# A second group pair by half products in three feed-forwards, products in another order, packed setup loads, and collecting copies on ScalarE

## Chip, cores and metric

One NeuronCore of a Trainium2 chip runs the whole program. The time is device microseconds of one execution. The kernel before takes 1335.24 us, the median of 3 runs (1333.88 to 1336.06).

## The reference

Two layers over 256 tokens of width 1024, in float32. Each layer has two feed-forwards (width 2816), three attention branches (differential, sparse, windowed) whose outputs are gated and merged, and a gated embedding term. The change touches the feed-forwards and the constants that the attention needs:

```python
def swiglu(x, wi, wo):
    gate, up = jnp.split(x @ wi, 2, axis=-1)
    return (jax.nn.silu(gate) * up) @ wo
...
for i in range(DEPTH):
    h = h + 0.5 * swiglu(rms_norm(h, norm_g[i, 0]), ffn1_wi[i], ffn1_wo[i])
    ...   # three attention branches, merged, added to h
    h = h + 0.5 * swiglu(rms_norm(h, norm_g[i, 2]), ffn2_wi[i], ffn2_wo[i])
    h = h + jax.nn.sigmoid(rms_norm(h, norm_g[i, 3]) @ w_ple_gate[i]) * (p[i] @ w_ple[i])
```

## The kernel before

A float32 product is made of three matmuls: each operand is split into a rounded high part and the remainder (`split`, L228 on ScalarE and L223 on VectorE), and `mul3` adds high by high, high by low and low by high (L235, L236, L237). Each weight comes from memory once as a tile of 128x1024 (512 KB, tile `raw`, four buffers); ScalarE writes its high part `wh`, VectorE the low part `wl` (six buffers each). So VectorE and ScalarE each do one instruction per weight tile before TensorE may use it.

A feed-forward has 11 groups of 256 gate and 256 up columns. The 256 tokens are two blocks t of 128. A plain group is 4 lines, one per weight tile; a line is 12 matmuls of 512 columns (2 depth blocks, 2 token blocks, 3 parts). Groups 8 and 9 are made together by half products (`Seven`, `seven`): the products of a 2x2 block matrix by 7 instead of 8 block products, each 4 depth blocks x 3 parts, again 12 matmuls. For these VectorE subtracts weight tiles from one another (`minus`; `x` and `y` are held tiles of two weight tiles each, filled through the GpSimd queue, L296), and adds the results (`plus`, L611, L624). `lines` says by a list `kinds` in which order lines of plain groups (0) and half products (1) come.

Each line's result goes through `gated`: Silu on ScalarE (`act`, L547), a multiplication on VectorE (L549), and, once 512 columns are there, `turn_by_dma`: ScalarE puts the two 16-bit halves of the numbers apart (`cut`, L516), the SP queue transposes them by DMA (`flip`, L517), VectorE puts them together (`whole`, L521) and `split` makes `gT`, the operand of the second product `fo`. `setup` loads constants and is run beside the lines of the first feed-forward at three fixed lines.

A planner with its own idea of time sets the order of the instructions on each engine; engines, and the SP queue that issues nearly all transfers, work strictly in that order.

Of the kernel before, what the change touches and what calls it, by code (L numbers as in the profile page):

```python
# [32 lines left out]
WBUFS = 6  # L33
PACE_A, PACE_B, PACE_C = 0.75, 0.72, 0.6
# [41 lines left out]
def _stream(i, x):  # L76
# [4 lines left out]
    def ffn(n, wi, wo):  # L81
        for f in range(FG):
            s = slice(256 * f, 256 * f + 256)
            yield f"{n}{f}", _subs(np.concatenate([wi[:, :DFF][:, s], wi[:, DFF:][:, s]], 1), 2)
        for c in range(2):
            yield f"{n}o{c}", _subs(wo[:, 512 * c:512 * c + 512], 2)
# [49 lines left out]
def _constants():  # L136
# [16 lines left out]
            "fold": np.tile(np.eye(32, dtype=np.float32), (2, 1))}  # L153

# [32 lines left out]
def trunk(ctx: ExitStack, tc: tile.TileContext, a: dict, out: bass.AP, index: list):  # L187
# [88 lines left out]
    class Seven:  # L276


        order = ("11", "t1", "t2", "t3", "22", "21", "t4")

        def __init__(self, i, fa, fb, x, y):
# [3 lines left out]
            self.at = {}  # L285

# [5 lines left out]
        def fill(self, n, into=None):  # L292
            f, first = self.src[n]
            p = where[self.i, f][0] + first
            if into is not None:
                nc.gpsimd.dma_start(into.rearrange("p (j n) -> p j n", j=2), a["wst"][p:p + 2].rearrange("j p n -> p j n"))  # L296
# [8 lines left out]
        def minus(self, n, x, y):  # L305
            self.raw[n] = self.raw[y]
            for j in range(2):
                sub(self.raw[y][j], self.raw[x][j], self.raw[y][j])

        def make(self, n):  # L310
            if n == "11":
                self.fill("11", self.x())
            elif n == "t1":
                self.fill("12", self.y())
                self.minus("t1", "12", "11")
# [3 lines left out]
            elif n == "t3":  # L319
                self.minus("t3", "22", "12")  # L320
            elif n == "21":
                self.fill("21")
            elif n == "t4":
                self.minus("t4", "21", "t2")
            self.tiles[n] = []
            for raw in self.raw[n]:
# [3 lines left out]
                self.tiles[n].append((hi, lo))  # L330

# [178 lines left out]
    def turn_by_dma(pool, src, m):  # L510
# [3 lines left out]
        flip = pool.tile([128, 2, 4, 128], U16, tag="flip", bufs=3, name="flip")  # L514
# [4 lines left out]
        def collect():  # L519
# [6 lines left out]
    def ffn(i, n, norm, after, aside=None):  # L526
# [10 lines left out]
        def collect(t, all=False):  # L537
            while pending[t] and (all or pending[t][0][0] <= now[0]):
                _, first, m, whole = pending[t].pop(0)
                split(gT[t][:, 0, first:first + m, :], gT[t][:, 1, first:first + m, :], whole())  # L540

        def gated(f, t, x):
            first = f - f % 2
            if (first, t) not in held:
                held[first, t] = [pool.tile([128, 512], F32, tag="gated", bufs=4, name="gated"), 0]
            act = pool.tile([128, 256], F32, tag="act", bufs=3, name="act")
            nc.scalar.activation(act, x[:, :256], AF.Silu, scale=norm.r(t))  # L547
            to = held[first, t]
            nc.vector.tensor_tensor(to[0][:, 256 * (f % 2):256 * (f % 2) + 256], act, x[:, 256:], op=ALU.mult)  # L549
            to[1] += 1  # L550
            if to[1] == 2 or f == FG - 1:
                pending[t].append((now[0] + 3, 2 * first, 2 * to[1], turn_by_dma(pool, to[0], 2 * to[1])))

        def gathered(t, k):
            if k == 8:
                collect(t, True)
# [46 lines left out]
        def seven(fa, fb, w):  # L603
# [10 lines left out]
            p1, p5, p6, p7 = y_bank("p1"), tp_bank("p5"), tp_bank("p6"), tp_bank("p7")  # L614
# [8 lines left out]
            with tc.high_priority(offset=150):  # L623
                nc.vector.tensor_tensor(v, v, p6, op=ALU.add)  # L624
            yield
            times(p7, sums[3], "t3", True)
            with tc.high_priority(offset=150):
                x = plus("w", v, p7)
                gated(fb, 1, plus("c22", x, p5))
            yield  # L630
# [804 lines left out]
```

## Time and profile before

| | |
|---|---|
| median of 3 runs | 1335.24 us |
| the profiled execution | 1335.53 us, span 1333.8 us |
| TensorE busy | 99%, 6366 matmuls |
| VectorE, ScalarE busy | 75%, 63% |
| VectorE busy in the lines of the second feed-forward | 94.19 of 117.90 us |

The span is the time from the first to the last instruction; 1.7 us of the execution lie around it. A matmul's busy time in the profile (some 390 ns) overlaps that of its neighbours, so the distance between two starts is the measure of TensorE's speed, not the busy time. In the same way an instruction of VectorE or ScalarE starts before the one ahead of it has ended.

### The profile page before, as it was taken

What the parts mean: (1) busy time and instruction counts of PE and PEld (TensorE: products, weight loads), DVE (VectorE), ACT (ScalarE), POOL (GpSimd) and SP (SyncE); (2) the same over time, 40 slices, a digit from 0 to 9 for tenths busy, and PEclk for the clock granted to TensorE, in tenths of its full rate; (3) what the DMA queues carried; (4) which work ended last, traced back from release to release, by engine and by line L of the source; (5) the groups of instructions that cost most, each with busy time, mean ns of one, the idle gap of its engine ahead of it and who ended that gap; (6) DMA issues with size and microseconds to landing.
All of it is one profiled execution on the core that took longest, in us unless ns stands there. A gap on an engine that the chain in (4) does not pass through costs nothing.

```text
span 1333.8 us, 17981 instructions
## 1 busy us (share of the span) xinstructions
PE 1314.9 (99%) x6366; PEld 1082.6 (81%) x6366; DVE 1004.5 (75%) x1693; ACT 834.5 (63%) x1375; POOL 28.6 (2%) x44
## 2 busy tenths in 40 slices
PE   9999999999999999999999999999999999999997
PEld 6868888887887788888888888888888878888886
DVE  7868756668979787776788776667688888868665
ACT  6657645659757575664666665467695656657544
POOL 1000000000000000000000000000000000000000
PEclk9999999999999999999999999999999999999999
DMA  8658855355653575786666685744546436668762
GB/s 333 186 167 252 250 194 202 131 174 175 213 171 111 172 223 158 226 241 192 209 204 190 205 244 189 243 152 150 185 154 219 157 95 224 189 184 223 237 213 71
DMA packets 120327, 257.12 MB, mean 193 GB/s; under 512 B 55280, under 2 KB 60836, under 8 KB 120238
## 3 DMA queue, kind: packets, MB, share of 16 engines
q1 hardware_dynamic: 117310, 245.95, 59.4%
q0 software_dynamic: 2496, 9.47, 2.1%
q8 instruction: 50, 0.82, 0.3%
q10 hardware_dynamic: 432, 0.56, 0.1%
q14 instruction: 39, 0.32, 0.1%
HBM read 243.33 MB, written 1.08 MB: 183 GB/s over the span
## 4 chain that ended last, share of the span: by engine, by line
PE 88%; DVE 4%; DMA 3%; ACT 2%; issue 2%; SPq 0%; POOLq 0%; POOL 0%; DVEq 0%; ACTq 0%
PE ff L236 8%; PE ff L237 8%; PE ff L235 8%; PE fo L235 6%; PE fo L237 6%; PE fo L236 6%; PE gate L235 3%; PE gate L237 3%; PE gate L236 3%; DMA raw<-in_wst 3%; PE s L725 2%; DVE wl L223 2%; PE A L237 2%; PE A L235 2%; PE A L236 2%
## 5 line engine op out<-in xcount | busy, mean ns | idle before, releaser
L223 DVE TENSOR_TENSOR wl<-raw,wh 128x1024 fp32r<-128x1024 f32 (+2 forms) x432 | 520.0, 1212 | 164.5 <-ACT wh L228 158.9
L228 ACT ACTIVATE wh<-raw 128x1024 fp32r<-128x1024 f32 (+2 forms) x432 | 450.4, 1049 | 240.4 <-DMA raw<-in_wst 86.8
L236 PE MATMUL ff<-wl,nT 128*128 128x512 f32 x576 | 225.4, 393 | 1.2 <-DVE wl L223 1.1
L237 PE MATMUL ff<-wh,nT 128*128 128x512 f32 x576 | 224.2, 391 | 0.6 <-DVE nT L223 0.6
L235 PE MATMUL ff<-wh,nT 128*128 128x512 f32 x576 | 221.9, 392 | 2.6 <-ACT wh L228 1.7
L237 PE MATMUL fo<-wh,gT 128*128 128x512 f32 x352 | 133.8, 390 | 0.0
L236 PE MATMUL fo<-wl,gT 128*128 128x512 f32 x352 | 133.7, 390 | 0.0
L235 PE MATMUL fo<-wh,gT 128*128 128x512 f32 x352 | 133.1, 391 | 0.0
L236 PEld LDWEIGHTS ff<-wl,nT 128*128 128x128 f32 x576 | 108.7, 189 | 26.7 <-DVE wl L223 3.6
L235 PEld LDWEIGHTS ff<-wh,nT 128*128 128x128 f32 x576 | 108.4, 189 | 27.0 <-ACT wh L228 3.1
L237 PEld LDWEIGHTS ff<-wh,nT 128*128 128x128 f32 x576 | 108.7, 189 | 23.2 <-DVE nT L223 0.9
L237 PEld LDWEIGHTS fo<-wh,gT 128*128 128x128 f32 x352 | 66.1, 188 | 13.6
L236 PEld LDWEIGHTS fo<-wl,gT 128*128 128x128 f32 x352 | 66.1, 188 | 13.5
L235 PEld LDWEIGHTS fo<-wh,gT 128*128 128x128 f32 x352 | 66.1, 188 | 13.5
L235 PE MATMUL gate<-wh,nT 128*128 128x512 f32 x192 | 76.8, 400 | 0.0
L236 PE MATMUL gate<-wl,nT 128*128 128x512 f32 x192 | 76.3, 397 | 0.0
L237 PE MATMUL gate<-wh,nT 128*128 128x512 f32 x192 | 75.9, 395 | 0.0
L736 ACT ACTIVATE p<-p,st 128x128 f32<-128x128 f32 (+1 forms) x128 | 56.6, 446 | 6.3 <-DVE st L734 6.0
L228 ACT ACTIVATE gT<-whole 128x512 fp32r<-128x512 f32 (+1 forms) x48 | 28.3, 589 | 36.3 <-DVE whole L521 36.2
L521 DVE COPY whole<-flip 128x1024 uint16<-128x1024 uint16 (+1 forms) x48 | 33.9, 706 | 21.2 <-DMA flip<-cut 20.9
L516 ACT ACTIVATE cut<-gated 128x1024 uint16<-128x1024 uint16 (+1 forms) x48 | 44.7, 976 | 1.1 <-DVE gated L549 0.6
L235 PEld LDWEIGHTS gate<-wh,nT 128*128 128x128 f32 x192 | 36.1, 188 | 8.3 <-ACT wh L228 0.3
(339 smaller groups left out, 2367.7 us busy)
## 6 DMA issues: line engine op xcount, KB each, us to landing
raw<-in_wst SPq DMA_DIRECT2D x422, 512.0 KB, 4.4
band<-table SPq DMA_DIRECT2D x10, 512.0 KB, 5.0
x<-in_wst POOLq DMA_DIRECT2D x4, 1024.0 KB, 7.4
y<-in_wst POOLq DMA_DIRECT2D x4, 1024.0 KB, 7.1
raw<-in_wbv SPq DMA_DIRECT2D x4, 420.0 KB, 3.2
xt<-in_xt SPq DMA_DIRECT2D x4, 256.0 KB, 5.3
raw<-in_wst SPq DMA_DIRECT2D x4, 256.0 KB, 4.5
h<-in_x SPq DMA_DIRECT2D x2, 512.0 KB, 7.7
```

The costliest lines, as they stand in the source:

```text
L223: nc.vector.tensor_tensor(o, x, y, op=ALU.subtract)
L228: nc.scalar.activation(hi, src, AF.Copy)
L235: nc.tensor.matmul(ps, xh, wh, start=start, stop=False, **kw)
L236: nc.tensor.matmul(ps, xh, wl, start=False, stop=False, **kw)
L237: nc.tensor.matmul(ps, xl, wh, start=False, stop=stop, **kw)
L516: nc.scalar.activation(cut.rearrange("p (w n) -> p w n", w=2), halves(src)[:, :128 * m].rearrange("p n w -> p w n"), AF.Copy)
L521: tc.keep_in_program_order(nc.vector.tensor_copy(halves(whole)[:, :128 * m].rearrange("p n w -> p w n"), flip.rearrange("p (w a) b -> p w ...
L725: nc.tensor.matmul(o, q[r, x, qb[m], t * 128:(t + 1) * 128], kk, start=x + y == 0, stop=x == 1)
L736: nc.scalar.activation(p[j], p[j], AF.Exp, bias=st[:, j:j + 1], scale=-1.0, accum_out=st[:, n + j:n + j + 1])
```

## The change

- The weights of a pair of groups are stored as 512 gate columns and 512 up columns, so Silu and the multiplication work on 512 columns (`opened_by`, `closed`); group 10 stays as it was.
- In the three feed-forwards without `setup` two pairs, groups 2, 3 and 4, 5, are made by half products; in the first one, as before, the pair 8, 9.
- The order of the seven products is 11, t1, t2, 22, t3, 21, t4. Block 12 is filled ahead into the held tile y (`begin`; SP queue in the first feed-forward, GpSimd queue in the others), block 11 comes as ordinary raw tiles, and t1 is written to x. Another bank and a sum `u` are used. `spread` places the half products among the plain lines by a list of VectorE costs.
- `collect` waits five lines instead of three, takes what `fo` needs next, and the copy `whole` runs on ScalarE except near the end of the lines.
- Nine setup loads become two (`late`, `kept`), and setup's parts are run at lines 10, 25 and 35 instead of 17, 22 and 33.

```diff
     class Seven:
-        order = ("11", "t1", "t2", "t3", "22", "21", "t4")
+        order = ("11", "t1", "t2", "22", "t3", "21", "t4")
+        then = {"11": ("t1", "12", "11"), "22": ("t3", "22", "12"), "21": ("t4", "21", "t2")}
...
+        def begin(self):
+            self.fill("12", self.y())
...
         def minus(self, n, x, y):
-            self.raw[n] = self.raw[y]
+            into = [self.x()[:, SUB * j:SUB * j + SUB] for j in range(2)] if n == "t1" else self.raw[y]
             for j in range(2):
-                sub(self.raw[y][j], self.raw[x][j], self.raw[y][j])
+                sub(into[j], self.raw[x][j], self.raw[y][j])
+            self.raw[n] = into
...
+            if n in self.then:
+                self.minus(*self.then[n])
+            if n == "t3" and self.following:
+                self.following.begin()
@@
-            tc.keep_in_program_order(nc.vector.tensor_copy(
-                halves(whole)[:, :128 * m].rearrange("p n w -> p w n"), flip.rearrange("p (w a) b -> p w (a b)", w=2)))
+            tc.keep_in_program_order(nc.vector.tensor_copy(to, of) if late else nc.scalar.activation(to, of, AF.Copy))
@@
+        def opened_by(f, t, x):
+            held[f // 2, t] = pool.tile([128, 512], F32, tag="gated", bufs=5, name="gated")
+            m = 256 if f == FG - 1 else 512
+            nc.scalar.activation(held[f // 2, t][:, :m], x[:, :m], AF.Silu, scale=norm.r(t))
+
+        def closed(f, t, x):
+            g, m = held.pop((f // 2, t)), 256 if f == FG - 1 else 512
+            nc.vector.tensor_tensor(g[:, :m], g[:, :m], x[:, 512 - m:], op=ALU.mult)
+            pending[t].append((now[0] + 5, 4 * (f // 2), m // 128, turn_by_dma(pool, g, m // 128)))
@@
+        def spread(half, whole):
+            cost = [5.0, 2.5, 6.3, 5.6, 3.2, 5.6, 3.9] * (half // 7)
...
-            groups = [iter([0, 1, 2, 3, 4, 5, 6, 7, 10]), iter([(8, 9)])]
+            if aside:
+                groups = [iter([0, 1, 2, 3, 4, 5, 6, 7, 10]), [(8, 9)]]
+                kinds = spread(7, 36)
+            else:
+                groups = [iter([0, 1, 6, 7, 8, 9, 10]), [(2, 3), (4, 5)]]
+                kinds = spread(14, 28)
@@
-                if aside and at in (17, 22, 33):
+                if aside and at in (10, 25, 35):
                     beside()
@@
+        late = pool.tile([128, sum(n for _, n in LATE)], F32, name="late")
+        fetched_late(nc.sync, late, a["late"])
+        fetched_late(nc.sync, kept, a["kept"])
```

Three places show how instructions move. The first is VectorE in the second feed-forward, where its first half products begin. `x` and `y` are the two held tiles, `raw` the weight tiles as they come, `wl` the low parts; numbers tell buffers apart. Before:

```order
L223 TENSOR_TENSOR wl_4623<-raw_4621,wh_4622 128x1024
L223 TENSOR_TENSOR wl_4641<-raw_4639,wh_4640 128x1024
L549 TENSOR_TENSOR gated_4569<-act_4570,ff0_4489 128x256
L549 TENSOR_TENSOR gated_4579<-act_4580,ff1_4502 128x256
L223 TENSOR_TENSOR wl_4675<-x_4672,wh_4674 128x1024
L223 TENSOR_TENSOR wl_4679<-x_4672,wh_4678 128x1024
L223 TENSOR_TENSOR x_4672<-y_4790,x_4672 128x1024 x2
L223 TENSOR_TENSOR wl_4697<-raw_4695,wh_4696 128x1024
```

And now:

```order
L242 TENSOR_TENSOR x_4435<-y_4436,raw_4565 128x1024
L242 TENSOR_TENSOR x_4435<-y_4436,raw_4567 128x1024
L242 TENSOR_TENSOR wl_4570<-raw_4565,wh_4569 128x1024
L242 TENSOR_TENSOR wl_4574<-raw_4567,wh_4573 128x1024
L242 TENSOR_TENSOR wl_4593<-raw_4591,wh_4592 128x1024
L242 TENSOR_TENSOR wl_4632<-x_4435,wh_4631 128x1024
L242 TENSOR_TENSOR wl_4636<-x_4435,wh_4635 128x1024
L573 TENSOR_TENSOR gated_4517<-gated_4517,ff0_4527 128x512
L242 TENSOR_TENSOR x_4435<-raw_4690,x_4435 128x1024
L242 TENSOR_TENSOR y_4436<-raw_4690,y_4436 128x1024
L573 TENSOR_TENSOR gated_4525<-gated_4525,ff1_4540 128x512
L242 TENSOR_TENSOR wl_4655<-raw_4653,wh_4654 128x1024
```

The subtraction that makes t1 now stands ahead of the low parts of block 11, and two subtractions that read block 22 straight from a raw tile (`raw_4690`) stand ahead of the low part of the next plain tile.

The second place is VectorE a little later in the same feed-forward, now (before has nothing like it so early): block 21 (`raw_4850`, `raw_4852`) is subtracted ahead of the low parts of two plain tiles that were asked for earlier.

```order
L242 TENSOR_TENSOR wl_4756<-raw_4690,wh_4755 128x1024
L242 TENSOR_TENSOR wl_4760<-raw_4692,wh_4759 128x1024
L242 TENSOR_TENSOR wl_4783<-y_4436,wh_4782 128x1024
L651 TENSOR_TENSOR v_4630<-v_4630,p6_4629 128x512
L242 TENSOR_TENSOR wl_4787<-y_4436,wh_4786 128x1024
L638 TENSOR_TENSOR u_4753<-v_4630,p5_4628 128x512
L242 TENSOR_TENSOR x_4435<-raw_4850,x_4435 128x1024
L242 TENSOR_TENSOR x_4435<-raw_4852,x_4435 128x1024
L242 TENSOR_TENSOR wl_4807<-raw_4805,wh_4806 128x1024
L242 TENSOR_TENSOR wl_4830<-raw_4828,wh_4829 128x1024
```

Block 22's raw tiles stay held from the subtractions of the first place until the first two rows here.

The third place is the SP queue around the setup loads of the first feed-forward. Before:

```order
L342 DMA raw<-in_wst 128x1024 x3
L517 DMA_TRANSPOSE flip<-cut 128x8x128 x2
L1302 DMA onehot<-in_onehot 32x384
L1302 DMA dead<-in_dead 20x384
L1302 DMA relb<-in_relb 32x20
L1302 DMA cmask<-in_cmask 128x32
L1302 DMA hmask<-in_hmask 128x8
L1302 DMA fold<-in_fold 64x32
L1302 DMA nsink<-in_sinks 128x16
L1302 DMA subln<-in_subln 128x2
L1302 DMA lamp<-in_lamp 128x512
L342 DMA raw<-in_wst 128x1024 x9
```

And now:

```order
L321 DMA y<-in_wst 128x2x1024
L365 DMA raw<-in_wst 128x1024 x3
L327 DMA raw<-in_wst 128x1024 x2
L365 DMA raw<-in_wst 128x1024
L1357 DMA late<-in_late 128x1302
L1357 DMA kept<-in_kept 128x88
L365 DMA raw<-in_wst 128x1024
L540 DMA_TRANSPOSE flip<-cut 128x8x128
L365 DMA raw<-in_wst 128x1024
L540 DMA_TRANSPOSE flip<-cut 128x8x128
```

Two loads stand where nine stood, earlier, ahead of the first transposes instead of behind the second pair; the held tile y is now filled from this queue.

## Rows read from the trace of the kernel before

**Rows 1.** The page: span, busy time of the engines, and the clock granted to TensorE in 40 slices.

```profile
span 1333.8 us, 17981 instructions
PE 1314.9 (99%) x6366; PEld 1082.6 (81%) x6366; DVE 1004.5 (75%) x1693; ACT 834.5 (63%) x1375; POOL 28.6 (2%) x44
PEclk9999999999999999999999999999999999999999
```

**Rows 2.** Busy time in stretches, here the lines of the four feed-forwards, from the first to the last matmul `ff`. Columns: stretch and its length, PE, PEld, DVE, ACT and POOL busy with counts, clock, DMA share, GB/s.

```profile
5.00:134.00 129.00, 124.26 (x521) 97.96 (x521) 101.63 (x136) 83.71 (x110) 5.55 (x7) 0.99 0.75 238
463.40:581.30 117.90, 117.90 (x525) 97.59 (x524) 94.19 (x118) 76.74 (x98) 2.54 (x4) 1.00 0.72 208
671.20:789.20 118.00, 118.00 (x526) 97.68 (x525) 96.55 (x117) 77.21 (x98) 2.11 (x4) 1.00 0.72 214
1117.80:1235.80 118.00, 118.00 (x526) 97.68 (x525) 95.23 (x118) 76.50 (x98) 2.52 (x4) 1.00 0.73 208
```

**Rows 3.** The timeline of TensorE in the second feed-forward: start, duration, instruction.

```profile
471.14 0.39 PE L236 MATMUL ff<-wl,nT 128*128 128x512 f32 x1
471.37 0.39 PE L237 MATMUL ff<-wh,nT 128*128 128x512 f32 x1
471.59 0.39 PE L235 MATMUL ff<-wh,nT 128*128 128x512 f32 x1
```

**Rows 4.** Busy time in stretches of the first feed-forward, with the columns of rows 2.

```profile
60.00:80.00 20.00, 17.77 (x75) 13.28 (x74) 11.84 (x25) 10.43 (x13) 0.62 (x2) 1.00 0.55 126
80.00:100.00 20.00, 19.22 (x82) 14.63 (x81) 12.39 (x14) 11.33 (x14) 1.45 (x2) 1.00 0.59 198
100.00:120.00 20.00, 19.71 (x86) 15.78 (x85) 16.84 (x20) 11.99 (x15) 0.00 (x0) 1.00 0.83 253
```

**Rows 5.** The timeline of the SP queue in the first feed-forward: start, time with the queue's waits, transfer.

```profile
62.73 3.58 SPq L517 DMA_TRANSPOSE flip<-cut  x2
...
70.42 0.43 SPq L1302 DMA_DIRECT2D lamp<-in_lamp  x1
70.96 28.50 SPq L342 DMA_DIRECT2D raw<-in_wst  x9
```

**Rows 6.** The timeline of VectorE in the first feed-forward; the bracket is the idle time ahead and what ended it.

```profile
66.94 0.76 DVE L521 COPY whole<-flip 128x1024 uint16<-128x1024 uint16 x1 [3.87 <-DMA flip<-cut]
75.91 0.43 DVE L1331 TENSOR_TENSOR lamp<-lamp 128x256 f32<-128x256 f32 x1 [3.11 <-DMA lamp<-in_lamp]
```

**Rows 7.** DMA issues of the first 140 us: transfers, KB each, median us from issue to landing.

```profile
raw<-in_wst SPq DMA_DIRECT2D x47, 512.0 KB, 4.9
lamp<-in_lamp SPq DMA_DIRECT2D x1, 256.0 KB, 5.5
```

**Rows 8.** Groups of VectorE's instructions in the lines of the second feed-forward (463.4 to 581.3), by form: count, busy time, mean ns, idle time ahead and what ended it.

```profile
L223 DVE TENSOR_TENSOR wl<-raw,wh 128x1024 fp32r<-128x1024 f32 x39 | 47.3, 1219 | 13.8 <-ACT wh L228 13.6
L521 DVE COPY whole<-flip 128x1024 uint16<-128x1024 uint16 x9 | 6.8, 755 | 4.6 <-DMA flip<-cut 4.6
L549 DVE TENSOR_TENSOR gated<-act,ff 128x256 f32<-128x256 f32 x16 | 6.2, 413 | 0.2
L223 DVE TENSOR_TENSOR x<-raw,x 128x1024 f32<-128x1024 f32 x4 | 4.9, 1218 | 3.5 <-DMA raw<-in_wst 3.5
```

**Rows 9.** The timeline of VectorE in the second feed-forward, and one row of the third.

```profile
473.03 0.68 DVE L566 TENSOR_TENSOR sum<-xg 128x512 f32<-128x512 f32 x1
...
477.71 2.35 DVE L223 TENSOR_TENSOR wl<-raw,wh 128x1024 fp32r<-128x1024 f32 x2
480.21 0.79 DVE L549 TENSOR_TENSOR gated<-act,ff 128x256 f32<-128x256 f32 x2
...
494.76 0.69 DVE L223 TENSOR_TENSOR gT<-whole,gT 128x512 fp32r<-128x512 f32 x1
495.37 0.75 DVE L521 COPY whole<-flip 128x1024 uint16<-128x1024 uint16 x1
496.01 2.34 DVE L223 TENSOR_TENSOR wl<-x,wh 128x1024 fp32r<-128x1024 f32 x2
...
505.98 1.22 DVE L223 TENSOR_TENSOR wl<-raw,wh 128x1024 fp32r<-128x1024 f32 x1
507.11 1.22 DVE L223 TENSOR_TENSOR x<-raw,x 128x1024 f32<-128x1024 f32 x1
...
686.45 0.68 DVE L566 TENSOR_TENSOR sum<-xg 128x512 f32<-128x512 f32 x1
```

**Rows 10.** Groups of ScalarE's instructions in the same lines, with the columns of rows 8.

```profile
L228 ACT ACTIVATE wh<-raw 128x1024 fp32r<-128x1024 f32 x39 | 40.8, 1056 | 21.7 <-DMA raw<-in_wst 12.7 <-PE ff L237 5.0 <-PE p L237 2.8
L516 ACT ACTIVATE cut<-gated 128x1024 uint16<-128x1024 uint16 x9 | 9.0, 1048 | 0.1
L547 ACT ACTIVATE act<-ff,stats 128x256 f32<-128x256 f32 x16 | 7.1, 467 | 3.5 <-PE ff L237 3.5
```

**Rows 11.** The timeline of the GpSimd queue in the second feed-forward.

```profile
467.97 0.75 POOL L296 DMA_DIRECT2D x<-in_wst  x1
474.28 0.72 POOL L296 DMA_DIRECT2D y<-in_wst  x1 [5.56 <-DVE sum L566]
```

**Rows 12.** The page: median us from issue to landing of a weight tile and of a held tile.

```profile
raw<-in_wst SPq DMA_DIRECT2D x422, 512.0 KB, 4.4
x<-in_wst POOLq DMA_DIRECT2D x4, 1024.0 KB, 7.4
```

More of the change, by code (lines that the diff above doesn't have):

```diff
@@ L33 @@
 WBUFS = 6
+FIRST, LAST = 7, 3
 PACE_A, PACE_B, PACE_C = 0.75, 0.72, 0.6
@@ L153, in _constants, with _packed @@
             "fold": np.tile(np.eye(32, dtype=np.float32), (2, 1))}
+LATE = [("lamp", 512), ("subln", DEPTH), ("onehot", REV), ("dead", REV), ("relb", NB)]
+KEPT = [("cmask", 32), ("hmask", 8), ("fold", 32), ("sinks", 8 * DEPTH)]
+def _packed(host):
+    host["lamp"] = np.broadcast_to(host["lamp"].reshape(1, -1), (128, 512))
+    host["sinks"] = np.broadcast_to(host["sinks"].reshape(1, -1), (128, 8 * DEPTH))
+    for name, parts in (("late", LATE), ("kept", KEPT)):
+        rows = [host.pop(n) for n, _ in parts]
+        host[name] = np.concatenate([np.concatenate([r, np.zeros((128 - len(r), r.shape[1]), np.float32)], 0) for r in rows], 1)
+    return host
 class Flow:
@@ L535, in begin, with collect @@
                 gT[t] = pool.tile([128, 2, NF, 128], F32R, name=f"gT{t}")
[L537 to L540, printed above, removed]
-        def gated(f, t, x):
[L543 to L552, printed above, removed]
+        def collect(t, upto=0):
+            for entry in [e for e in pending[t] if e[1] <= upto or e[0] <= now[0]]:
+                pending[t].remove(entry)
+                _, first, m, whole = entry
+                split(gT[t][:, 0, first:first + m, :], gT[t][:, 1, first:first + m, :], whole(now[0] > len(ahead) - 6))
+        def opened_by(f, t, x):
[6 more added lines that the diff above has]
+            pending[t].append((now[0] + 5, 4 * (f // 2), m // 128, turn_by_dma(pool, g, m // 128)))
+        def gated(f, t, x):
+            if f % 2 == 0:
+                opened_by(f, t, x)
+            if f % 2 or f == FG - 1:
+                closed(f, t, x)
         def gathered(t, k):
-            if k == 8:
-                collect(t, True)
+            collect(t, k + 4)
             return gT[t][:, 0, k, :], gT[t][:, 1, k, :]
@@ L1278, in trunk, with columns @@
     ident = base.tile([128, 128], F32, name="ident")
[L1279 to L1285 removed]
+    small = base.tile([128, 8], F32, name="small")
+    mhalf, nlam, sg = small[:, :4], small[:, 4:4 + DEPTH], small[:, 4 + DEPTH:4 + 2 * DEPTH]
+    kept = base.tile([128, sum(n for _, n in KEPT)], F32, name="kept")
+    def columns(x, parts):
+        at = 0
+        for _, n in parts:
+            yield x[:, at:at + n]
+            at += n
+    cmask, hmask, fold, nsink = columns(kept, KEPT)
+    cmask, fold = cmask.rearrange("p (t n) -> p t n", t=2), fold[:64]
+    nsink = nsink.rearrange("p (d n) -> p d n", d=DEPTH)
     cbias = base.tile([128, NT, 8, 16], F32, name="cbias")
```

105 lines of the change are left out of this document (50 added, 55 removed).

## The prediction

> **What bounds the kernel now.** I read the page first: TensorE is busy for 99% of the span at full clock, VectorE for 75% [rows 1]. Then the stretches of the four feed-forwards' lines [rows 2]. Such a stretch holds 432 matmuls of the plain groups and 84 of the half products. Two starts lie 0.2267 us apart (471.14 to 471.59 is two steps) [rows 3], so 516 matmuls need 117.0 us; the second to fourth feed-forward take 117.9 to 118.0 us, the rest being transposes between them. TensorE does not wait there at all, and only fewer matmuls can shorten them. The first takes 128.5 us (129.0 less half a microsecond of margin): some 11 us are waits, of which those at the very start are not touched here. Later, 20 us would hold 88 matmuls, and the stretches from 60 to 120 us held 75, 82 and 86 [rows 4]: 13 + 6 + 2 are missing, 21 x 0.2267 = 4.8 us, half a microsecond of it setup's own matmul. There the SP queue stood behind two transposes and nine small loads from 62.73 to 70.96, with no weight asked for [rows 5], while VectorE stood 3.87 us for a transposed tile and 3.11 us for `lamp` [rows 6].
>
> VectorE is the nearest rival for the bound: 94.19 of 117.90 us in the second feed-forward [rows 2], with 13.6 us of its idle time before `wl` spent on ScalarE's `wh` [rows 8], which in part itself waits for TensorE to give buffers back [rows 10]. It is ahead, not late.
>
> **The change, part by part.** *Matmuls.* A second pair by half products is 84 instead of 96 matmuls: 12 x 0.2267 = 2.72 us, three times: 8.2 us. Nothing beside it, since TensorE is the bound: this is the gain.
>
> *VectorE in the three feed-forwards.* The distance between starts, not the duration, counts: 1.135 us for 1024 columns (505.98 to 507.11), 0.61 for 512 (494.76 to 495.37), 0.64 for `whole` (495.37 to 496.01), 0.37 for a multiplication of 256 (two in 0.79 us) [rows 9]. Low parts go from 36 + 14 = 50 to 28 + 28 = 56: +6.8 us. Subtractions of weight tiles go from 8 to 16: +9.1. Sums of results go from 5 to 10: +3.1. Multiplications, 22 of 256, become 10 of 512 and 2 of 256: 8.1 to 6.8, -1.3. Of nine copies `whole` in the stretch [rows 8] about three stay: -3.9. In all +13.8: 108.0 us in a stretch that should last 117.9 - 2.7 = 115.2, so 94% instead of 80%. ScalarE gets six high parts at 1.06 us (6.3), eight copies at 1.05 (8.4, below), one more `v` of 512 columns (half of it, 0.5) and saves some 2 on Silu, whose 22 instructions of 0.47 become 10 of twice the width and 2 [rows 10]: 76.7 to about 90, 78%, no bound. A copy on ScalarE has no row here; `cut`, the same move the other way, takes 1.05 us [rows 10] against 0.76 for VectorE's `whole` [rows 8], so more than 0 and up to twice `cut` each; I take the near row, 1.05. Twice that would be 98 of 115.2 us, still no bound.
>
> The Trainium skill, ScalarE: Activation LUTs, section Rules for kernel authors, says that simple element work belongs on VectorE, not ScalarE. The rows agree on the price of one copy, yet by that rule six more copies on VectorE, 3.9 us, would put it at 111.9 of 115.2 us; the sum above stands without it.
>
> *Is VectorE in time?* I add up its instructions in the new order against what TensorE needs. In the second feed-forward the last sum of activations starts at 473.03 and ends its turn at 473.6 [rows 9]; up to there the order is as before. Two low parts and three half-width ones take it to 477.7, which is where the trace has it. The held tile y lies now where x lay, so it can be asked for when x was, at 467.97, and with 7.4 us to land it is there by 475.4 [rows 11, 12]; no wait. Two subtractions and two low parts bring the first tile of the half products at 481.1 and the second at 482.3; TensorE, 8 lines of 2.72 after 463.4 and some displaced work, wants them at 483.1 and 484.5. The lead is about 2 us. Five more rows and the first read of block 22 follow (first place shown): its raw buffer comes free at 482.3 and lands 4.4 us later [rows 12], 486.7, against 486.3: a wait of half a microsecond. The plain tile that ends the first fence is done at 490.9, wanted at 491.8; the next one at 494.3, wanted at 494.5. At the second place block 21's buffers are the plain tiles', and the queue reaches them behind two loads whose buffers come free at 502.0 and 503.1 with block 22's low parts: four tiles land one behind the other, the third at about 508.5, VectorE is there at 506.6, waits 1.9 us, and the plain tile behind it is done at 512.1 where TensorE wants it at 510.8: a stall of 1.3 us. In the second pair the margins are of the same size. So I expect a stall of 1.5 us per feed-forward, 4.5 in all. The bounds: nothing, if those loads land two microseconds sooner than the median, and 5 us per feed-forward, if every such read waits as long as those of before (3.5 us for four reads in two places [rows 8], 1.75 each; six places are 10.5 us, against 7.2 us that VectorE has free and a lead of 2). In the third feed-forward the last sum comes at 686.45, 15.2 us after the lines began at 671.2 instead of 9.6 [rows 9]; fewer instructions stand behind it, and I give it no price of its own.
>
> *Setup and the first feed-forward.* Its matmuls stay 516. Seven issues of about half a microsecond leave SP (66.36 to 70.96 for nine: 4.6 us, now about 1) [rows 5]. `late` is 128 x 1302 numbers, 667 KB, against 256 for `lamp`, which took 5.5 us [rows 7]; it is asked for some 30 us earlier, and VectorE reads it after the next plain tile's low part, so it may wait as it does now, 3.1 us [rows 6], but the stretch's queue is not blocked by transposes at that moment. The copy `whole`, for which VectorE stood 3.87 us, is ScalarE's and two lines later. VectorE has less to do there than before. Of the 4.8 us I take 3.0 as returned; the bounds are -1 (`late` is waited for a microsecond longer than `lamp`, and nothing else is won) and 4.8.
>
> The Trainium skill, DMA: Bandwidth & Descriptors, section Anatomy of one DMA, gives each transfer about 2 us of fixed cost. Seven transfers fewer would by that be 14 us of transfers' time; the rows show 0.4 to 0.6 us of the queue for each and the landings beside one another, and I keep to those.
>
> *What moves elsewhere.* The order in the attention branches and in `fo` is nearly the same. The last pair's columns are needed by `fo` eight lines in, and its transposes are asked for before the lines end; I price this at nothing, 0 to 1 us.
>
> *The sum*, against the execution's 1335.5: -8.2 + 4.5 - 3.0 = -6.7, 1328.8. The execution lies 0.3 us above the median of 1335.2, so 1328.5 for the median.
>
> **The rivals.** *No stall at all* (B): the reads of raw tiles are hidden, and the first feed-forward gets all of its waits back: 1335.2 - 8.2 - 4.8 = 1322.2. For it: VectorE's 94% still leaves 7.2 us per stretch, and it starts ahead. Against: my ledger meets TensorE's need to within 1 us at three places of the first pair alone.
>
> *VectorE takes what TensorE gives* (C), no change: stalls of 2.7 us per feed-forward eat the 8.2, the first returns 0 to 2.5: 1332.7 to 1335.2, about 1334.5. For it: every wait of VectorE beyond its 7.2 us becomes TensorE's.
>
> *Raw buffers make it slower* (D). Only four weight tiles can be under way, and a pair of half products holds two of them from its subtractions to its low parts. If each of the six places costs a landing of 4.4 us less the two instructions of 1.135 that lie between, 2.1 us, VectorE's stretch is 108.0 + 12.6 = 120.6 us and sets the end: 2.7 over before, three times 8.1, less 1.5 for the first: about 1342. It decides from 1.65 us per place on (9.9 us, the free 7.2 and the 2.7 saved); the 1.75 of before lies there, but was measured where VectorE was ahead and asked early.
>
> **How the numbers follow.** My forecast (A) gets 0.50, with its own range of 1324 to 1332.5; B 0.17, C 0.16, D 0.17. A time within 0.2%, 2.7 us, cannot be told from no change. Faster is A and B, 0.67; same is C, 0.16; slower is D, 0.17. The range for 8 in 10 goes from 1320, under B, to 1339, which takes in C and the near side of D.
>
> **What would show it.** 6330 matmuls; the lines of the second to fourth feed-forward at 115.2 us plus the stalls, which I expect as waits of TensorE on `wl` behind a VectorE that waited for `raw`; VectorE at some 108 us there; in the first feed-forward a stretch of about 125.5 instead of 128.5, with no gap of the SP queue at the setup loads. I am wrong if those three stretches exceed 118 us (then D, and the waits must stand at reads of `raw`), or if VectorE is far from 108 us, which would make my count of its work wrong, or if the first stretch is longer than before.

## The result, and the profile after

The changed kernel takes 1322.99 us (median of 4 runs, 1322.52 to 1324.46) against 1335.26 us before (4 runs, 1333.88 to 1336.06): ratio 0.9911, 95% interval 0.9894 to 0.9928. That is 12.3 us less; 6.7 were predicted. The profiled execution took 1322.82 us, and 2.4 us of it lie around the span.

The page of the changed kernel, answering [rows 1]:

```profile
span 1320.4 us, 17921 instructions
PE 1304.1 (99%) x6330; PEld 1075.1 (81%) x6330; DVE 1038.8 (79%) x1686; ACT 873.1 (66%) x1380; POOL 26.3 (2%) x42
```

6366 - 6330 = 36 matmuls fewer. The stretches of the feed-forwards' lines, with the columns of [rows 2]:

```profile
5.00:127.90 122.90, 120.69 (x520) 96.94 (x520) 99.14 (x122) 90.85 (x111) 4.17 (x5) 1.00 0.84 263
457.80:573.00 115.20, 115.20 (x513) 95.38 (x512) 108.75 (x121) 89.71 (x102) 2.54 (x4) 1.00 0.72 217
663.00:778.70 115.70, 115.70 (x515) 95.76 (x515) 107.36 (x116) 86.65 (x98) 2.13 (x4) 1.00 0.72 216
1107.20:1222.50 115.30, 115.30 (x514) 95.40 (x513) 109.28 (x122) 90.75 (x104) 2.50 (x4) 1.00 0.73 218
```

The second to fourth feed-forward took 117.9, 118.0 and 118.0 us and now take 115.2, 115.7 and 115.3: 2.7 + 2.3 + 2.7 = 7.7 us. In these rows PE's busy time equals the length of the stretch, so TensorE did not wait at all, though VectorE is busy for 108.75 of 115.2 us. From its first matmul `ff` to the first `fo` (5.1 to 133.6 before, 5.1 to 127.9 now) the first feed-forward went from 128.5 to 122.8 us, 5.7 less. Together that is 13.4 us, the whole difference of the spans (1333.8 - 1320.4): in sum nothing came from elsewhere. The profiled executions differ by 12.7 us only, since 2.4 us lie around the span instead of 1.7; no run here shows why. The stretches of the first feed-forward, answering [rows 4]:

```profile
60.00:80.00 20.00, 20.00 (x90) 16.55 (x89) 12.83 (x15) 13.47 (x16) 0.00 (x0) 1.00 0.69 193
80.00:100.00 20.00, 20.00 (x87) 15.76 (x86) 15.82 (x22) 14.29 (x16) 2.25 (x3) 1.00 0.81 208
100.00:120.00 20.00, 20.00 (x90) 16.55 (x89) 15.18 (x16) 17.52 (x21) 0.00 (x0) 1.00 0.83 275
```

Where 75, 82 and 86 matmuls stood there are now 90, 87 and 90 (a row also counts the matmuls that cross its ends, so a full one shows 90): 24 more at 0.2267 us, 5.4 of the 5.7 us. Only setup's own matmul, between 80 and 100, leaves a dent.

VectorE's groups in the lines of the second feed-forward (457.8 to 573.0), answering [rows 8]:

```profile
L242 DVE TENSOR_TENSOR wl<-raw,wh 128x1024 fp32r<-128x1024 f32 x40 | 47.7, 1218 | 3.2 <-ACT wh L247 3.2
L242 DVE TENSOR_TENSOR x<-raw,x 128x1024 f32<-128x1024 f32 x8 | 9.8, 1222 | 1.5 <-DMA raw<-in_wst 1.5
L242 DVE TENSOR_TENSOR y<-raw,y 128x1024 f32<-128x1024 f32 x4 | 4.9, 1219 | 0.8 <-DMA raw<-in_wst 0.8
```

The reads of raw tiles waited for 1.5 + 0.8 = 2.3 us in six places, 0.4 us each, where before two places had cost 3.5 us. In the group of low parts of raw tiles the wait for ScalarE's high parts fell from 13.6 to 3.2 us: that was most of VectorE's spare time. Some 6 us of it are left in the stretch (115.2 - 108.75).

ScalarE's groups there, answering [rows 10]:

```profile
L247 ACT ACTIVATE wh<-raw 128x1024 fp32r<-128x1024 f32 x39 | 41.0, 1058 | 16.4 <-DMA raw<-in_wst 7.9 <-PE ff L256 5.7 <-PE p L256 1.8
...
L539 ACT ACTIVATE cut<-gated 128x1024 uint16<-128x1024 uint16 x10 | 10.4, 1045 | 1.3 <-DVE gated L573 1.3
L545 ACT ACTIVATE whole<-flip 128x1024 uint16<-128x1024 uint16 x6 | 7.9, 1370 | 0.0
```

### The profile page after: what moved, and what is told of

Same layout as the page of the kernel before. It is cut to its first block, busy times and chain, and to the rows that moved or that the text cites. A ratio compares the mean times of both kernels' runs of the same rounds, so it can differ in the third digit from the quotient of the medians.

```text
span 1320.4 us, 17921 instructions
## 1 busy us (share of the span) xinstructions
PE 1304.1 (99%) x6330; PEld 1075.1 (81%) x6330; DVE 1038.8 (79%) x1686; ACT 873.1 (66%) x1380; POOL 26.3 (2%) x42
## 4 chain that ended last, share of the span: by engine, by line
PE 94%; DVE 3%; issue 1%; ACT 1%; DMA 0%; POOL 0%; SPq 0%; POOLq 0%; DVEq 0%; ACTq 0%
PE ff L255 8%; PE ff L256 8%; PE ff L254 8%; PE fo L256 6%; PE fo L255 6%; PE fo L254 6%; PE p L254 3%; PE p L256 3%; PE p L255 3%; PE gate L254 3%; PE gate L256 3%; PE gate L255 3%; PE s L774 2%; PE br L254 2%; PE A L256 2%; PE A L254 2%
## 5 line engine op out<-in xcount | busy, mean ns | idle before, releaser
L242 DVE TENSOR_TENSOR wl<-raw,wh 128x1024 fp32r<-128x1024 f32 (+1 forms) x434 | 519.6, 1211 | 146.3 <-ACT wh L247 142.1
L247 ACT ACTIVATE wh<-raw 128x1024 fp32r<-128x1024 f32 (+1 forms) x434 | 452.0, 1050 | 242.9 <-DMA raw<-in_wst 85.0
L255 PE MATMUL ff<-wl,nT 128*128 128x512 f32 x480 | 186.9, 391 | 1.0 <-DVE wl L242 1.0
L256 PE MATMUL ff<-wh,nT 128*128 128x512 f32 x480 | 186.4, 390 | 0.6 <-DVE nT L242 0.6
L254 PE MATMUL ff<-wh,nT 128*128 128x512 f32 x480 | 178.9, 391 | 0.6 <-ACT nT L434 0.6
L255 PEld LDWEIGHTS ff<-wl,nT 128*128 128x128 f32 x480 | 90.2, 188 | 20.8 <-DVE wl L242 2.2
L254 PEld LDWEIGHTS ff<-wh,nT 128*128 128x128 f32 x480 | 90.2, 188 | 20.8 <-ACT nT L434 1.8
L256 PEld LDWEIGHTS ff<-wh,nT 128*128 128x128 f32 x480 | 90.2, 188 | 19.6 <-DVE nT L242 0.9
L255 PEld LDWEIGHTS fo<-wl,gT 128*128 128x128 f32 x352 | 66.1, 188 | 13.6
L254 PEld LDWEIGHTS fo<-wh,gT 128*128 128x128 f32 x352 | 66.1, 188 | 13.6
L256 PEld LDWEIGHTS fo<-wh,gT 128*128 128x128 f32 x352 | 66.1, 188 | 13.6
L242 DVE TENSOR_TENSOR wl<-x,wh 128x1024 fp32r<-128x1024 f32 x42 | 50.6, 1218 | 2.7 <-ACT wh L247 2.3
L247 ACT ACTIVATE wh<-x 128x1024 fp32r<-128x1024 f32 x42 | 43.8, 1050 | 6.2 <-DVE x L242 4.5
L255 PE MATMUL p<-wl,xs 128*128 128x512 f32 x112 | 43.6, 389 | 0.0
```

What stands on the lines that cost most here:

```text
L242: nc.vector.tensor_tensor(o, x, y, op=ALU.subtract)
L247: nc.scalar.activation(hi, src, AF.Copy)
L254: nc.tensor.matmul(ps, xh, wh, start=start, stop=False, **kw)
L255: nc.tensor.matmul(ps, xh, wl, start=False, stop=False, **kw)
L256: nc.tensor.matmul(ps, xl, wh, start=False, stop=stop, **kw)
```

## Experiments

All are edits of the changed kernel but the last two, which are edits of the kernel before. A lead is the time from the end of a low part on VectorE to TensorE's start on the same weight tile. The theories after the result: TensorE lost its 36 matmuls and VectorE's lead covered everything else (the lead theory), against a lead so thin that the spacing and the moved copies were needed to keep it; and for the first feed-forward, the place of setup, the number of its loads, or the copies.

**One pair again.** The three later feed-forwards go back to one pair, all else as changed.

```diff
-                groups = [iter([0, 1, 6, 7, 8, 9, 10]), [(2, 3), (4, 5)]]
-                kinds = spread(14, 28)
+                groups = [iter([0, 1, 4, 5, 6, 7, 8, 9, 10]), [(2, 3)]]
+                kinds = spread(7, 36)
```

> The changed kernel, but with one pair of groups by half products (2, 3) in the three later feed-forwards too; all else of the change stays. Theory: the three feed-forwards gained by fewer matmuls alone, 36 x 0.2267 us, so with them back the lines last 118.0, 118.4 and 118.0 us instead of 115.2, 115.7 and 115.3, and the whole takes 1323.0 + 8.1 = 1331. Rival: the new order, the wider gate instructions and the copies on ScalarE brought the gain there; then the time stays within 2 us of 1323.

Measured: 1332.6 us, ratio to before 0.998 (0.997 to 0.9989). Its stretches of the later feed-forwards:

```profile
457.80:575.80 118.00, 118.00 (x526) 97.70 (x525) 90.34 (x102) 81.75 (x95) 1.82 (x3) 1.00 0.75 216
666.50:784.40 117.90, 117.90 (x525) 97.62 (x524) 92.73 (x102) 83.42 (x96) 1.42 (x3) 1.00 0.75 220
1113.60:1231.60 118.00, 118.00 (x526) 97.67 (x525) 92.13 (x105) 83.96 (x98) 1.79 (x3) 1.00 0.75 218
```

118.0 us each, as before the change, and 9.6 us of the 12.3 are gone from the time. Of these, 2.8 + 2.2 + 2.7 = 7.7 us stand in the three stretches; the rest is a longer `fo`, the second product, in each of the three (61.2 instead of 60.6 us in the second feed-forward). The second pair is the larger part of the gain, and in the lines its price is that of the matmuls, 7.7 against 8.2 us reckoned.

**All copies on VectorE.**

```diff
-            tc.keep_in_program_order(nc.vector.tensor_copy(to, of) if late else nc.scalar.activation(to, of, AF.Copy))
+            tc.keep_in_program_order(nc.vector.tensor_copy(to, of))
```

> The changed kernel, but every collecting copy on VectorE. Some eight copies of 0.64 us come back to VectorE in each of the three later feed-forwards: 108.7 + 5.1 = 113.8 busy of 115.2 us. Theory that VectorE's lead was small (its waits at raw tiles, 0.2 to 0.9 us each, just fit): lines of 117 to 119 us there, 1329 to 1334 in all. Rival, that the lead was ample and the move of the copies was not needed: lines within 0.7 us of 115.2, time within 2.5 us of 1323. In the first feed-forward, where VectorE is busy for 99 of 123 us, both expect less than 1.5 us.

Measured: 1324.71 us, ratio 0.9918 (0.9903 to 0.9933), which cannot be told from the changed kernel. The second feed-forward's lines:

```profile
457.80:573.40 115.60, 115.60 (x515) 95.70 (x514) 109.25 (x124) 79.81 (x93) 2.54 (x4) 1.00 0.72 213
```

No stall. VectorE's busy time hardly grows within the lines: it makes seven copies there instead of one, but other work of it slid out of them (38 low parts of raw tiles instead of 40, six halves of `gT` instead of seven). ScalarE is relieved by 10 us, which nobody needed.

**Three raw tiles instead of four** (`RAWS = 3`).

> The changed kernel with three buffers for raw weight tiles instead of four. The rival of the prediction in which raw buffers make the change slower: with a pair holding two of the three, each of the six places per feed-forward waits a whole landing of 4.4 us less what lies between, 2 us or more, 12 us per feed-forward and 1355 or more in all, with waits of VectorE on raw at the subtractions. Theory that the reads are asked for early enough: a buffer less costs one tile's turn of about 1.7 us at some places, lines of 116 to 119 us, 1326 to 1338.

Measured: 1395.75 us, ratio 1.0452 (1.043 to 1.0474). The second feed-forward's lines, and the longest wait of ScalarE and VectorE in them (engine, line, releaser: us in total, times, longest):

```profile
484.20:612.50 128.30, 120.38 (x514) 95.66 (x513) 107.59 (x120) 88.53 (x100) 2.54 (x4) 0.99 0.65 195
```

```profile
ACT wh L247 <- DMA raw<-in_wst: 30.7, 18, 5.7
```

```profile
DVE wl L242 <- ACT wh L247: 13.4, 11, 2.8
DVE x L242 <- DMA raw<-in_wst: 5.3, 6, 1.7
```

The later feed-forwards lose 13, 9 and 14 us, the size that this run's expectation gave for the rival of raw buffers (12 us), but one buffer further down; and the wait stands first at ScalarE's high parts and only for 5.3 us at VectorE's subtractions. The other half of the 73 us lies outside these stretches, 18 us of it in the first feed-forward (140.9 instead of 122.8 us). VectorE is busy for only 107.59 of 128.30 us: a total that fits did not prevent this stall.

**A third pair.**

```diff
-                groups = [iter([0, 1, 6, 7, 8, 9, 10]), [(2, 3), (4, 5)]]
-                kinds = spread(14, 28)
+                groups = [iter([0, 1, 8, 9, 10]), [(2, 3), (4, 5), (6, 7)]]
+                kinds = spread(21, 20)
```

> The changed kernel with a third pair (6, 7) by half products in the three later feed-forwards. 36 matmuls fewer: if TensorE stayed the bound, lines of 112.5 us and 1315. But VectorE would get 6 low parts, 8 subtractions, 5 sums more and 22 - some multiplications less: 108.7 + 17.6 = 126 us. Theory that VectorE is the next bound and has 6 us left: lines of 126 to 129 us, VectorE over 96% busy, 1355 to 1365. Rival, that the lines are bound by waits at raw tiles before VectorE is full: longer still, over 131, with VectorE under 93%.

Measured: 1378.68 us, ratio 1.0324 (1.0304 to 1.0345). The three stretches, and in the first of them TensorE's longest wait and VectorE's wait for raw tiles:

```profile
457.60:590.40 132.80, 120.76 (x502) 92.83 (x501) 126.13 (x139) 94.25 (x108) 3.26 (x5) 0.99 0.61 187
680.20:816.20 136.00, 123.23 (x503) 94.89 (x501) 129.33 (x139) 94.97 (x108) 2.84 (x5) 0.96 0.61 189
1146.10:1278.00 131.90, 119.44 (x502) 91.55 (x501) 127.77 (x141) 95.13 (x110) 3.21 (x5) 1.00 0.63 191
```

```profile
PEld p L255 <- DVE wl L242: 10.3, 11, 1.5
```

```profile
DVE x L242 <- DMA raw<-in_wst: 1.5, 2, 1.3
```

VectorE is busy for 126.13 of 132.8 us and TensorE waits for its low parts. This is the wait of TensorE that the prediction had expected one pair earlier, but behind a VectorE that is full, not behind one that waits for raw tiles (1.5 us). Neither expectation was met in size: the lines are longer than the theory's 126 to 129 us and the time 14 us over its range, while VectorE is at 95 to 97% and not under the rival's 93%. So the next step in the same direction is closed: VectorE's work per pair (17.4 us here, 126.13 - 108.75) no longer fits beside fewer matmuls.

**Even spacing.** `spread` spaces the half products evenly, not by VectorE's time.

```diff
-            cost = [5.0, 2.5, 6.3, 5.6, 3.2, 5.6, 3.9] * (half // 7)
-            more = [c - 2.0 for c in cost]
+            more = [1.0] * half
```

> The places of the half products among the plain products are spread evenly instead of by VectorE's time. If VectorE's lead is small and the spacing by its time is what keeps TensorE fed, the three later feed-forwards show stalls behind wl: 1 to 2 us each, 117 us instead of 115.2, in all 1326 to 1329. If the lead is ample (rival, as the move of the copies to VectorE suggested), nothing changes: stretches of 115.2 to 115.7 and 1322 to 1324.

Measured: 1323.72 us, ratio 0.9921 (0.9908 to 0.9935): not to be told from the changed kernel. The lines of the second and the fourth feed-forward stay at 115.3 us, but the third one's lines take 117.2 instead of 115.7 us:

```profile
663.00:780.20 117.20, 116.45 (x515) 95.59 (x514) 106.29 (x116) 86.77 (x99) 2.13 (x4) 1.00 0.71 208
```

```profile
743.20 1.22 DVE L242 TENSOR_TENSOR wl<-x,wh 128x1024 fp32r<-128x1024 f32 x1 [2.20 <-ACT wh L247]
```

TensorE's longest wait there, 1.1 us, is for this low part, which VectorE made late because it had waited 2.20 us for ScalarE's high part. So in this execution the spacing by VectorE's time is worth 1.5 us in one stretch of three and nothing in the others; it is not what keeps TensorE fed in general.

**Setup at its old lines.**

```diff
-                if aside and at in (10, 25, 35):
+                if aside and at in (17, 22, 33):
```

> The setup stands at the lines where it stood before (17, 22, 33), its loads still packed into two. If the 5.7 us that the first feed-forward returned come from the number of loads, its lines stay at about 123 us and the whole at 1323. If they come from the place (loads ahead of the lines in which SP issues the transposes), some 3 us come back: lines of 126 us and 1326.

Measured: 1323.24 us, ratio 0.9919 (0.9906 to 0.9933).

**Nine loads at the new lines.** `late` and `kept` come in nine transfers of columns, the same bytes.

```diff
-        fetched_late(nc.sync, late, a["late"])
-        fetched_late(nc.sync, kept, a["kept"])
+        for tile_, name, parts in ((late, "late", LATE), (kept, "kept", KEPT)):
+            at = 0
+            for _, n in parts:
+                fetched_late(nc.sync, tile_[:, at:at + n], a[name][:, at:at + n])
+                at += n
```

> The same bytes in the same place of the program, but late and kept are loaded by nine transfers of columns instead of two. If the number of loads was the cost (seven more issues of SP at half a microsecond, 3.5 us in which no weight is asked for), the first feed-forward's lines grow from 122.8 to 125 or 126 us: 1325 to 1326. If the place was what counted, they stay within a microsecond: 1323.

Measured: 1323.23 us, ratio 0.9921 (0.9907 to 0.9934).

**Both at once**, nine loads at the old lines.

> Both at once: nine loads, and setup at lines 17, 22 and 33 as before. Alone, the place moved the 60 to 80 us stretch from 90 to 82 matmuls and the number of loads moved nothing. If the two are a cost only together (SP held up by the nine loads just behind two transposes), that stretch falls to about 75 to 78 matmuls as before and the first feed-forward's lines grow to about 126 to 127 us: 1326. If they are not the cause, it stays at 82 and the lines at 124: 1324.

Measured: 1324.96 us, ratio 0.9925 (0.991 to 0.9939).

**Both, and the old collecting in the first feed-forward**: three lines after the transpose, on VectorE.

```diff
-                split(gT[t][:, 0, first:first + m, :], gT[t][:, 1, first:first + m, :], whole(now[0] > len(ahead) - 6))
+                split(gT[t][:, 0, first:first + m, :], gT[t][:, 1, first:first + m, :], whole(aside or now[0] > len(ahead) - 6))
-            pending[t].append((now[0] + 5, 4 * (f // 2), m // 128, turn_by_dma(pool, g, m // 128)))
+            pending[t].append((now[0] + (3 if aside else 5), 4 * (f // 2), m // 128, turn_by_dma(pool, g, m // 128)))
```

> As the run with nine loads at the old lines, and in the first feed-forward alone the transposed tiles are collected three lines after they are asked for instead of five, by VectorE instead of ScalarE. If VectorE standing at a tile not yet there (3.87 us in the kernel before) was the third part of the cost, the lines reach 127 to 128.5 us, near the 128.5 of before: 1327 to 1329. If the collecting time does not matter, it equals the run with the old setup alone.

Measured: 1323.36 us, ratio 0.9913 (0.9897 to 0.993). The stretch from 60 to 80 us with setup late, with both, and with both and the old collecting:

```profile
60.00:80.00 20.00, 19.56 (x82) 14.59 (x81) 13.07 (x20) 12.57 (x15) 0.71 (x1) 1.00 0.64 184
```

```profile
60.00:80.00 20.00, 19.55 (x83) 14.87 (x82) 12.64 (x20) 12.89 (x15) 0.71 (x1) 1.00 0.65 170
```

```profile
60.00:80.00 20.00, 20.00 (x88) 15.75 (x87) 13.99 (x23) 11.45 (x15) 0.71 (x1) 1.00 0.70 182
```

82, 83 and 88 matmuls, with setup's own matmul in all three stretches, against 75 before and 90 in the changed kernel. The first feed-forward's lines take 124.1, 123.4 and 122.4 us, and 123.8 with nine loads at the new place, against 122.8 and, before, 128.5. Neither the place, nor the loads, nor the collecting, nor all three undone take the 5.7 us away again: these theories fell as sole causes.

**Two pairs in the first feed-forward too**, the version meant to beat both kernels.

```diff
-                groups = [iter([0, 1, 2, 3, 4, 5, 6, 7, 10]), [(8, 9)]]
-                kinds = spread(7, 36)
+                groups = [iter([0, 1, 2, 3, 8, 9, 10]), [(4, 5), (6, 7)]]
+                kinds = spread(14, 28)
```

> The first feed-forward too gets two pairs by half products, spread as in the others. By the price of matmuls alone (12 x 0.2267 = 2.7 us) its lines go from 122.8 to 120.1 us and the whole to 1320.3. If the wait for weights limits that stretch (it moves 263 GB/s where the others move 217) or VectorE, with about 14 us more work on 99, comes late, it gains nothing or loses: 1323 to 1328.

Measured: 1324.18 us, ratio 0.9932 (0.9919 to 0.9946): no better. One stretch shows where the gain is lost:

```profile
100.00:120.00 20.00, 18.79 (x78) 14.11 (x78) 19.83 (x21) 15.50 (x19) 0.00 (x0) 1.00 0.48 158
```

TensorE gets 78 matmuls through instead of 90, and these 12 are just the 12 saved. VectorE has no spare time in the stretch (19.83 of 20 us), but it comes into it late, behind ScalarE:

```profile
96.11 2.56 ACT L545 ACTIVATE whole<-flip 128x1024 uint16<-128x1024 uint16 x2
```

```profile
100.17 1.23 DVE L242 TENSOR_TENSOR wl<-raw,wh 128x1024 fp32r<-128x1024 f32 x1 [2.64 <-ACT wh L247]
```

ScalarE put two collecting copies ahead of a high part (99.09), for which VectorE waited 2.64 us. TensorE's weight loads then waited about as long for ScalarE's high parts (1.9 us) as for VectorE's low parts (1.6). Which of the two engines limits this version was not tried.

**The kernel before, setup early** (lines 10, 25 and 35, the nine loads as they were).

> The kernel before with one edit: setup stands at lines 10, 25 and 35, its nine loads as they were. If the place is what returned time in the first feed-forward, its lines fall from 128.5 to about 124 or 125 us: 1331. If the place counts only together with packing and later collecting, they stay at 127 to 128.5: 1334 to 1335.

Measured: 1331.85 us, ratio to before 0.9975 (0.9966 to 0.9984). The first feed-forward takes 125.0 us. Two of its stretches:

```profile
40.00:60.00 20.00, 18.32 (x81) 14.86 (x80) 20.00 (x27) 14.01 (x17) 0.00 (x0) 1.00 0.87 251
60.00:80.00 20.00, 20.00 (x90) 16.52 (x89) 14.79 (x19) 12.89 (x17) 0.00 (x0) 1.00 0.49 136
```

In the kernel before, the place alone is worth about 3.3 us (the interval of the ratio allows 2.1 to 4.5). The 15 missing matmuls between 60 and 80 us are all there, but 9 are missing 20 us earlier, where setup now meets the half products on a VectorE that is busy for 20.00 of 20 us. That makes 9 x 0.2267 = 2.0 us, about the rest to the changed kernel's 122.8.

**The kernel before with three raw tiles**, a control.

> A control for the run of the changed kernel with three raw tiles (1395.8, +73 us, its later feed-forwards +9 to +14 us): the kernel before with three. If half products need the fourth tile more than plain products do, before loses clearly less in those three stretches, 2 to 6 us each, and less in all. If any order of products suffers alike, it loses the same 9 to 14 us per stretch, about 1405.

Measured: 1453.29 us, ratio 1.0886 (1.0859 to 1.0914): 118 us lost, where the changed kernel loses 73. Two of its feed-forwards, a stretch of the first one, and ScalarE's wait in the second (498.2 to 639.3):

```profile
498.20:639.80 141.60, 126.19 (x520) 98.79 (x519) 92.58 (x114) 75.68 (x96) 2.54 (x4) 0.95 0.58 169
1210.80:1355.60 144.80, 127.71 (x525) 99.43 (x524) 94.72 (x117) 76.05 (x95) 2.52 (x4) 0.95 0.57 168
80.00:100.00 20.00, 14.78 (x41) 9.34 (x41) 7.31 (x13) 8.67 (x10) 2.08 (x3) 0.74 0.43 136
```

```profile
ACT wh L228 <- DMA raw<-in_wst: 46.5, 24, 5.9
```

Some 24 and 27 us are lost per stretch with one pair in the old order of products, 9 to 14 with two pairs in the new one. Both expectations missed: the changed kernel suffers less from the lack of the fourth tile, not more. Which part of the change does that (the first difference now goes into the held tile, the third one stands later) was not tried.

## Why the prediction was right, and where it was wrong

The time lies in the range of 1320 to 1339, but 1 us below the forecast's own range of 1324 to 1332.5. Two terms were off the same way, the stalls by 4.5 us and the first feed-forward by 2.7; with the matmuls 0.5 the other way the forecast of 6.7 becomes the 13.4 us of the spans. So the sign and the largest term were right for their reasons, and the middle of the forecast was not.

*Matmuls, -8.2 us: right.* The stretches fell by 7.7 us, and one pair again brings 7.7 back in them.

*VectorE's and ScalarE's work: right.* 108.0 us were reckoned and 108.75, 107.36 and 109.28 measured; for ScalarE about 90, and 89.71, 86.65 and 90.75 measured. One price was off: a collecting copy on ScalarE takes 1370 ns and not the 1.05 us of `cut` [rows 10], about 0.3 us each; that the sum came out is luck, since six copies fell into the stretch instead of the eight reckoned. Two rules that the prediction weighed would not have helped. The Trainium skill, ScalarE: Activation LUTs, section Rules for kernel authors, gives work such as add and mul to VectorE, which the prediction applied to copies: with all copies there no difference can be told, since TensorE waited for nothing in those lines either way. The Trainium skill, DMA: Bandwidth & Descriptors, section Anatomy of one DMA, sets about 2 us of fixed cost for a transfer that GpSimd issues; the loads of setup are issued by SP, and seven more of them there did not show in the time (1323.23 against 1322.99 us).

*Stalls of TensorE, +4.5 us: wrong, 0 measured.* The step that failed is the time at which the ledger lets TensorE want a tile. That sum is wrong as it stands: 8 lines of 2.72 us after 463.4 end at 485.2, and some displaced work comes on top, but 483.1 was written. The later wants were counted on from there, so all of them lie about a line, 2.7 us, too early. VectorE's low parts of block 11 and TensorE's first matmul of the half products:

```profile
474.43 3.49 DVE L242 TENSOR_TENSOR wl<-raw,wh 128x1024 fp32r<-128x1024 f32 x3
```

```profile
480.56 0.39 PE L254 MATMUL p<-wh,nT 128*128 128x512 f32 x1
```

The first low part was done 17.9 us after the lines' start (474.43 + 1.22 - 457.8), reckoned 17.7: the count of VectorE's work held. TensorE came to it after 22.8 us, reckoned 19.7: the lead was 4.9 us and not 2.

At the second place a smaller error came on top, the wait of 1.9 us for a raw tile. VectorE there, SP's loads for it, and TensorE at the plain tile behind it:

```profile
481.90 1.22 DVE L242 TENSOR_TENSOR x<-raw,x 128x1024 f32<-128x1024 f32 x1 [0.90 <-DMA raw<-in_wst]
...
501.51 2.49 DVE L242 TENSOR_TENSOR x<-raw,x 128x1024 f32<-128x1024 f32 x2 [0.19 <-DMA raw<-in_wst]
503.91 3.49 DVE L242 TENSOR_TENSOR wl<-raw,wh 128x1024 fp32r<-128x1024 f32 x3
```

```profile
489.43 6.52 SPq L365 DMA_DIRECT2D raw<-in_wst  x3
496.75 1.46 SPq L327 DMA_DIRECT2D raw<-in_wst  x2
```

```profile
507.76 0.61 PE L254 MATMUL ff<-wh,nT 128*128 128x512 f32 x2
```

VectorE got to the second place 43.5 us after the lines' start (501.51 - 0.19 - 457.8), reckoned 43.2. The tile was there at 501.51, 43.7 us after the start; I had it land at 508.5 - 463.4 = 45.1. It was asked for at 496.75 and came 4.8 us later, hardly slowed by the loads around it, where I had put four landings one behind the other. The low part of the plain tile behind it was done after 47.3 us (503.91 + 1.22), reckoned 48.7, and TensorE began on that tile, after its 24 matmuls for block 22 and t3, at 507.76, after 50.0 us, reckoned 47.4. So there was a lead of 2.6 us where the ledger had a stall of 1.3. Some 2.6 us of the difference are TensorE's want and some 1.4 the landing; with the want a line later even the wait of 1.9 us would have stalled nothing. The first place, at 481.90, waited 0.90 us (half a microsecond reckoned) and did not reach TensorE either.

So the waits measured at VectorE, up to 0.9 us, are inside a lead of 2.6 to 4.9 us. The copies on VectorE show this from a second side, the even spacing shows it in two stretches of three, and the third pair shows where it ends. The upper bound of 5 us per feed-forward does not follow from its numbers either: 10.5 us of waits against 7.2 free leave 3.3.

*The first feed-forward, -3.0 us: right in sign, mis-sized, 5.7 measured*, 0.9 more than the upper bound of 4.8. The loads of setup were asked for early and read without a wait. SP and VectorE in the changed kernel:

```profile
30.40 0.43 SPq L1357 DMA_DIRECT2D late<-in_late  x1
30.88 0.42 SPq L1357 DMA_DIRECT2D kept<-in_kept  x1
```

```profile
38.77 0.42 DVE L1378 TENSOR_TENSOR late<-late 128x256 f32<-128x256 f32 x1
```

The bound had counted 88 matmuls to a full 20 us, while a full row shows 90 by its own way of counting: 24 have come back between 60 and 120 us, not 21. I took 3.0 because I supposed that `late` would be waited for as `lamp` was [rows 6]. It was not, since it was asked for 8 us before its read.

What the runs settle of this term and what they don't: in the kernel before, the place of setup alone is worth 3.3 us. In the changed kernel the place, the number of loads and the collecting can all be undone and the time stays within 2 us. So the several edits to the first feed-forward cover for each other: their effects do not add. What is left as the difference is the rest of the change: the new order of the half products with their spacing, the wide multiplications and Silu, the packed tile, and the held tile y filled by SP. The spacing by itself is not it, since with the even one the first feed-forward takes 122.7 us; the others were not tried alone. One more thing stands in the trace. ScalarE in the kernel before, behind the last of nine loads:

```profile
73.47 1.28 ACT L1333 ACT_TABLE_LOAD   x1
76.83 0.20 ACT L1333 ACTIVATE lam<-lam 128x4 f32<-128x4 f32 x1 [2.07 <-DVE lam L1332]
77.21 1.06 ACT L228 ACTIVATE wh<-raw 128x1024 fp32r<-128x1024 f32 x1 [0.18 <-DMA raw<-in_wst]
```

The exponential for `lam` stood ahead of the next high part, and its input `lamp` was the ninth load. But it is not what held that high part, which waited another 0.18 us behind it, by the profile for its raw tile. That tile was asked for at 70.96, right behind `lamp` [rows 5], and was there 6.25 us later, at 77.21. In the run with all three undone, where `lamp`'s columns are the first of the nine, SP and ScalarE show:

```profile
69.44 19.05 SPq L365 DMA_DIRECT2D raw<-in_wst  x9
```

```profile
73.42 1.06 ACT L247 ACTIVATE wh<-raw 128x1024 fp32r<-128x1024 f32 x1 [1.33 <-DMA raw<-in_wst]
```

There the tile was asked for 1.5 us earlier and was there after 4.0 us. 77.21 - 73.42 = 3.8 us is of the size of what that run has more than the kernel before between 60 and 80 us (88 - 75 = 13 matmuls, 2.9 us), but `lamp`'s place in the queue was not tried alone, so this part stays open.

*The rivals.* "No stall at all" (1322.2) is what happened, within a microsecond (its terms of 8.2 and 4.8 came out as 7.7 and 5.7). I gave it 0.17 because my ledger met TensorE's need to within 1 us at three places; with TensorE's wants a line later the same ledger speaks for it. "VectorE takes what TensorE gives" and "raw buffers" did not happen: the reads waited 0.4 us per place, under the 1.65 from which the latter would have decided, and the control shows the changed kernel to lose less than the one before when a raw tile is taken away.

## What to carry to other kernels

When TensorE is busy for the whole of a stretch, price a removed matmul by the distance between two starts and believe it: that term came out within 0.5 us. A ledger of a helper engine was good for its total work (here to 1.5%) and for the times of its instructions (to 0.3 us up to the second place). It is worth as much as its other column, the times at which the bound engine wants the results: one line of 2.7 us miscounted there made a stall out of a lead. Check that column against the trace before trusting a margin of a microsecond. A margin of 6 us in 115 was enough here, and one of less than nothing cost 56 us; but a total that fits is not enough by itself, as the run with three raw tiles shows. When several edits attack the same stall, undo them both alone and together, in the old kernel and in the new: here one was worth 3.3 us in the old kernel and nothing that could be told in the time of the new one.

## What the hardware showed that I had not expected

The same copy of 16-bit halves costs ScalarE 1045 ns when it gathers them (`cut`) and 1370 ns when it scatters them (`whole`), and VectorE 755 ns [rows 8]. And a starved TensorE also slows down: in the control with three raw tiles, from 80 to 100 us, only 41 matmuls ran and the mean granted clock was 0.74 of full speed, so part of the stretch was at the lower of the two levels, 1.2 GHz; the stretch from 60 to 80 us ahead of it already had gaps (64 matmuls, clock 0.92), and in the one behind it as few matmuls ran at 0.86:

```profile
60.00:80.00 20.00, 16.26 (x64) 11.82 (x63) 14.64 (x20) 8.23 (x10) 0.00 (x0) 0.92 0.43 101
```

In the later feed-forwards of the changed kernel and of the one before the mean granted clock is 1.00, so there this cost nothing.
